# Mixer weight sums by accumulating transfers in DRAM, product banks alternated, operands fetched in double steps

## The chip, the cores and the metric

The kernel runs on one core of one Trainium2 chip. The metric is the device time of one execution in microseconds. A kernel is run several times and the median is given.

The core's engines each work through their own queue in order: PE (TensorE) does matmuls and transposes, DVE (VectorE) and ACT (ScalarE) elementwise work, POOL (GpSimd) elementwise work too, SP (SyncE) issues transfers. Engines wait for one another by semaphores. A DMA that an engine issues stands in that engine's queue until what it waits for has come.

## The reference, cut to what matters

One block on 1024 tokens of width 1024: an S5 state-space branch and a forgetting-attention branch, merged by gates, then one output projection, a cross-attention into 256 memory tokens, a SwiGLU feed-forward and norms.

```python
u = rms_norm(h, norm_mix)
u_ssm, q, k, v, f_logit, gate_logits = split(u @ w_in)
y_ssm = gelu(s5_ssm(u_ssm, ...))
glu_a, glu_b = split(y_ssm @ w_glu, 2)
out_a = glu_a * sigmoid(glu_b)
out_b = forgetting_attention(q, k, v, f_logit + b_forget) @ w_fox_o
gate_a, gate_b = split(sigmoid(gate_logits), 2)
h = h + (gate_a * out_a + gate_b * out_b) @ w_mix_out
h = h + memory_cross_attention(rms_norm(h, norm_mem_q), rms_norm(mem, norm_mem_kv), ...)
f_a, f_b = split(rms_norm(h, norm_ffn) @ w_ffn_in, 2)
h = h + (silu(f_a) * f_b) @ w_ffn_out
return rms_norm(h, norm_final)
```

The change concerns the line with `w_mix_out`, a product of 1024x1024 by 1024x1024, and what is prepared beside it.

## The kernel before, in words

All matrix products are done on fp32 values split in two: a rounded high part and the rest as low part. ACT casts the high part (L183) and DVE or POOL subtracts to get the low part (L184). One product of 128x128 by 128x512 is three matmuls: high by high, high by low, low by high. Small tiles are named `whi`/`wlo`, `moh`/`mol`, `wph`/`wpl` for such pairs.

The program's stages in order: the input norm and projections with the S5 branch, attention, the gated unit, the products of the output projection, cross-attention, feed-forward, final norm. What follows is what the change and the prediction touch. Line numbers are those of the kernel before, as in its profile.

*The start.* Tokens are normed, `w_in` is loaded by SP in pieces (`raw`, L158), the S5 inputs are stored to DRAM (`u_d<-us`, L515) and read back regrouped (`xg<-u_d`, L1594). POOL scales two token tiles (`xt`, L229) and then makes the S5 weights: `w`, `fre`, `fim` (L1523 to L1526), which PE transposes at L1569, powers `EC`, `ES` (L1555 to L1557), and small constants such as `r` (L1603) and `St` (L1632).

*The gated unit.* For each of eight blocks `j` of 128 channels, `Glu` makes `glu_a` by DVE (`sg<-mm`, L1328), the sigmoid of `glu_b` by ACT (`sb`, L1333), their product by DVE (L1334), and POOL multiplies by the gate `ga` that SP loads (`sg<-sg,ga`, L1341). `fox_part(j)` makes the attention's projection on PE in `pv` or `misc` banks (three matmuls, L173 to L175), multiplies it by the gate `gb` on DVE (L617) and adds (L620). Half tiles (`ga`, `gb`, `sb`) come from a small pool that is reused.

*The output projection* is Strassen's in Winograd's form. The merged activations and `w_mix_out` are cut into 2x2 blocks of 512x512, and seven products of blocks, numbered 1 to 7, are added into `H`, which holds `x` at first. The activation sums are made on DVE in `merged_pair` (L636 to L641). The weight sums for products 4 to 7 are made in the gated unit: `mix_fetch` loads rows of `w_mix_out`, `mix_sums` adds on POOL (L654), `mix_store` writes the sums to the DRAM tile `mt_d` (L659). Each product has four steps of 128 rows of the inner dimension (`p`), each step 4 x 3 matmuls of 128x512 (L703) that accumulate in four PSUM banks; behind the fourth step four DVE operations add the banks into `H` (L710). `m_get` fetches a step's operands: it loads one weight block (128x512) into `raw`, and splits the activation block with DVE and the weight block with POOL. The order of products is 1, 6, 7, 5, 4, 2, 3; product 1, 6, 5 use the banks sc, sc, mm, mm, products 7 and 4 use mm, misc, pv, pv, products 2 and 3 go by tiles or by the first set. Operands are fetched four steps ahead.

*Beside the products*, `ahead(j)` prepares tiles of the feed-forward weight `w_ffn_in`: SP loads two tiles (`wpr`), ACT and DVE split them, DVE makes five sums (L793 to L798), and ACT's queue stores the results to DRAM (`w_d`, L771). `ahead(0)` is woven among the products' steps, then come `ahead(1)` and `ahead(2)`, beside the last products, the norms and what follows.

*Order.* A scheduler places each instruction in its engine's queue by the order in the code, by what it depends on and by its own estimate, so what depends on nothing can stand far ahead of where the code writes it. `issue_after` (in `B.behind`) holds an instruction back.

Of the kernel before, what the change touches and what calls it, by code (L numbers as in the profile page):

```python
# [9 lines left out]
F32 = mybir.dt.float32  # L10
# [9 lines left out]
P = 128  # L20
# [289 lines left out]
def hybrid_block_kernel(ctx: ExitStack, tc: tile.TileContext, x, mem, norm_mix, w_in, b_forget,  # L310
# [30 lines left out]
    wg_d = B.dram.tile([4, P, 2 * D], F32, name="wg_d")  # L341
    glu = Glu(B, sh, yT, wg_d, gate_d)
    with tc.tile_pool(name="fox", bufs=1, reuse_waits="tile") as fp:
        fox = Fox(B, fp, sh, uT, w_in, b_forget[0], cum_d, rd_d, att_d)
        fox.run(y_d, yT, aT, w_glu, wg_d, [f for j in range(4) for f in glu.values(j)])
    glu.after = fox.maxima[NH - 2]
    with tc.tile_pool(name="st2", bufs=1, reuse_waits="tile") as s2:
        stage_tail(B, big, s2, sh, x, glu, aT, gate_d, kv_d, w_fox_o, w_mix_out, norm_mem_q[0], w_mem_q,
                   w_mem_o, norm_ffn[0], w_ffn_in, w_ffn_out, norm_final, out)
# [232 lines left out]
def stage_tail(B, big, s2, sh, x, glu, aT, gate_d, kv_d, w_fox_o, w_mix_out, g_mq, w_mem_q, w_mem_o, g_ffn,  # L582
# [7 lines left out]
    def slot(dt=F32, name="t"):  # L590
        return s2.tile([P, D], dt, tag="t", bufs=NS2, name=name)
# [10 lines left out]
    mt_d = B.dram.tile([8, 4, P, 512], F32, name="mt_d")  # L602
    mblk = {}

    def fox_part(j):
# [15 lines left out]
        if j % 2 == 0:  # L621
            gs[j // 2] = sg[:, :512]
        else:
            merged_pair(j // 2)

    def block(n, p):


        if p % 2 == 0 and (n, p) not in mblk:
            t_ = slot(name=f"m{n}")  # L630
            mblk[n, p], mblk[n, p + 1] = t_[:, :512], t_[:, 512:]
        return mblk[n, p]

    def merged_pair(p):
# [3 lines left out]
        V.tensor_sub(block(7, p), a11, a21)  # L638
# [3 lines left out]

    msum = {}

    def mix_fetch(p):
        msum[p] = slot(name="ws1"), slot(name="ws2")
        for i, t_ in enumerate(msum[p]):
            S.dma_start(t_, w_mix_out[(2 * p + i) * P:(2 * p + i + 1) * P, :])

    def mix_sums(p):  # L650
        w1, w2 = msum[p]
        b11, b12, b21, b22 = w1[:, :512], w1[:, 512:], w2[:, :512], w2[:, 512:]
        for o, i in ((b11, b12), (b12, b22), (b22, b11), (b21, b22)):
            G.tensor_add(o, o, i)  # L654

    def mix_store(p):
        w1, w2 = msum.pop(p)
        for n, o in ((5, w1[:, :512]), (7, w1[:, 512:]), (6, w2[:, 512:]), (4, w2[:, :512])):
            S.dma_start(mt_d[n, p], o)  # L659

    for j in range(8):
        if j > 3:
            with B.behind(glu.after):
                for f in glu.values(j):
                    f()
        glu.rest(j)
# [6 lines left out]
        if j > 2:  # L673
            fox_part(j - 3)
    H = [bslot(name=f"h{t}") for t in range(NT)]
    u2 = Act(s2, "t", NS2, 8, L, name="u2")
    MORDER = (1, 6, 7, 5, 4, 2, 3)
    mseq = [(n, p) for n in MORDER for p in range(4)]
    mops = {}

    def m_get(m):
        n, p = mseq[m]
        rb = B.wpool.tile([P, RAW], F32, tag="raw", bufs=4, name="raw")[:, :512]
        if n < 4:
            j, c = 2 * p + (n > 1), 512 * (n > 2)
            src = w_mix_out[j * P:(j + 1) * P, c:c + 512]
        else:
            src = mt_d[n, p]
        S.dma_start(rb, src)
        if m < 4:  # L690
            hl = [B.wpool.tile([P, WSLOT], F32R, tag=t_, name=t_)[:, :D] for t_ in ("whi", "wlo")]
        else:
            hl = bslot(F32R, "moh"), bslot(F32R, "mol")
# [4 lines left out]
    def m_mm(m, i, ps):  # L698
        n, p = mseq[m]
        hi, lo = mops[m]  # L700
        gi = slice(i * P, (i + 1) * P)
        for k, (l_, r_) in enumerate(((hi, hi), (hi, lo), (lo, hi))):
            T.matmul(ps, l_[:, gi], r_[:, 512:], start=k == 0 and p == 0 and n in (1, 2, 7),  # L703
                     stop=p == 3 and k == 2, skip_group_check=True)

    def m_add(n, i, ps):
        t, c, op = {1: (4, 0, ALU.add), 2: (4, 0, ALU.add), 6: (0, 0, ALU.add), 7: (0, 1, ALU.subtract),
                    5: (0, 1, ALU.subtract), 4: (0, 0, ALU.add), 3: (4, 1, ALU.subtract)}[n]
        h = H[t + i][:, 512 * c:512 * c + 512]
        return V.tensor_tensor(out=h, in0=h, in1=ps, op=op)  # L710

    msets = []

    def m_step(m):
        n, p = mseq[m]
        if m == 0:
            msets.append([B.bank(t_) for t_ in ("sc", "sc", "mm", "mm")])
        if m == 8:
            msets.append([B.bank(t_) for t_ in ("mm", "misc", "pv", "pv")])
        set_ = msets[n in (7, 4)]  # L720
        for i in range(4):
            m_mm(m, i, set_[i])
        if p == 3:
            for i in range(4):
                m_add(n, i, set_[i])

    def m_tile(i):
        ps = B.bank(("mm", "misc")[i % 2])
        for p in range(4):
            m_mm(20 + p, i, ps)  # L730
        m_add(2, i, ps)

    def m_x(t):
        S.dma_start(H[t], x[t * P:(t + 1) * P, :])

    MAHEAD = 4
    for t in range(4, NT):
        m_x(t)
    fox_part(5)
    for m in range(3):  # L740
        m_get(m)
    fox_part(6)
    m_get(3)
    m_step(0)
    m_step(1)
    for t in range(4):
        m_x(t)
    fox_part(7)
    m_get(4)
    m_get(5)  # L750
    gq = B.bcast_gain(s2, g_mq)

    def gemm_n(ps, act, t, w, nk):
        for k in range(nk):
            ah, al = act.tok(k, t)
            B.mm3(ps, ah, al, w[0][k], w[1][k], k == 0, k == nk - 1)

    def norm(t, gb, act, banks=("misc", "pv")):
        xs = s2.tile([P, D], F32, tag="xs", bufs=1, name="xs")
        B.norm_scale(xs, H[t], B.rstd(H[t]), gb)  # L760
        return B.norm_turn(xs, act, t, banks)

# [5 lines left out]
    def ahead(j):  # L768
# [53 lines left out]

    def m_next(m):
# [843 lines left out]
class Fox:  # L1667
# [280 lines left out]
    def run(self, y_d, yT, aT, w_glu, w_d, filler):  # L1948
# [54 lines left out]
        for h in range(NH):  # L2003
# [76 lines left out]
```

## Time and profile before

| | us |
|---|---|
| median of three runs | 1553.93 |
| the three runs | 1553.87, 1553.93, 1557.8 |
| the profiled execution | 1555.15 |
| its span in the trace | 1553.4 |
| PE busy in the span | 1518.3 |
| DVE busy | 1043.6 |
| ACT busy | 670.3 |
| POOL busy | 318.4 |
| PE's granted clock, mean | 0.993 of full |

The span is the traced part of the execution; 1.75 us of the profiled time lie outside it. A busy share is an average over stages with different limits, so the stretch from 540 to 800 us, in which the gated unit and the products run, is read by itself.

In rows of groups or lines of code, `L703 PE MATMUL sc<-moh` says: line 703, engine, operation, the tile written and the tile read. PEld is PE's loading of weights. A row of waits says which engine at which line waited, for which engine's work at which line, with total, count and longest wait in us. A row of the chain of waits gives the start, the duration and the work that something later waited for.

### The profile page before, as it was taken

What the parts mean: (1) busy time and instruction counts of PE and PEld (TensorE: products, weight loads), DVE (VectorE), ACT (ScalarE), POOL (GpSimd) and SP (SyncE); (2) the same over time, 40 slices, a digit from 0 to 9 for tenths busy, and PEclk for the clock granted to TensorE, in tenths of its full rate; (3) what the DMA queues carried; (4) which work ended last, traced back from release to release, by engine and by line L of the source; (5) the groups of instructions that cost most, each with busy time, mean ns of one, the idle gap of its engine ahead of it and who ended that gap; (6) DMA issues with size and microseconds to landing.
All of it is one profiled execution on the core that took longest, in us unless ns stands there. A gap on an engine that the chain in (4) does not pass through costs nothing.

```text
span 1553.4 us, 20548 instructions
## 1 busy us (share of the span) xinstructions
PE 1518.3 (98%) x7281; PEld 1251.6 (81%) x7281; DVE 1043.6 (67%) x1860; ACT 670.3 (43%) x1215; POOL 318.4 (20%) x385
## 2 busy tenths in 40 slices
PE   8999999999999997999899999999999999999998
PEld 7888888898777676887778888888888888888886
DVE  7936463346788855778866697777777776576555
ACT  7423333324667642124655564333333333354343
POOL 1166541100121218424402200000000000101001
PEclk9999999999999999999999999999999999999999
DMA  9734556611233747676630256445555543897652
GB/s 282 161 107 96 135 124 139 195 28 11 50 49 84 210 133 249 209 256 209 210 121 4 109 191 197 162 160 158 159 160 160 160 149 129 276 393 238 190 162 109
DMA packets 200454, 245.60 MB, mean 158 GB/s; under 512 B 36152, under 2 KB 128232, under 8 KB 199840
## 3 DMA queue, kind: packets, MB, share of 16 engines
q1 hardware_dynamic: 192864, 226.47, 49.0%
q10 hardware_dynamic: 7488, 17.83, 3.1%
q8 instruction: 57, 0.93, 0.2%
q14 instruction: 45, 0.37, 0.1%
HBM read 169.28 MB, written 76.91 MB: 158 GB/s over the span
## 4 chain that ended last, share of the span: by engine, by line
PE 84%; DVE 7%; DMA 3%; ACT 2%; issue 2%; POOL 2%; SPq 0%; POOLq 0%; ACTq 0%; DVEq 0%
PE mm L1054 15%; PE pv L1054 8%; PE mm L173 7%; PE mm L175 7%; PE mm L174 7%; PE mm L1197 5%; PE sc L1054 4%; PE sc L1197 4%; PE pv L1197 3%; PE sc L175 3%; PE sc L174 3%; PE sc L173 3%; PE misc L1197 2%; PE mm L703 1%; PE sc L1882 1%
## 5 line engine op out<-in xcount | busy, mean ns | idle before, releaser
L183 ACT CAST whi<-raw 128x1024 fp32r<-128x1024 f32 (+2 forms) x120 | 107.1, 895 | 112.2 <-PE mm L174 39.1
L184 DVE TENSOR_TENSOR wlo<-raw,whi 128x1024 fp32r<-128x1024 f32 (+2 forms) x116 | 121.7, 1055 | 40.4 <-ACT whi L183 39.3
L184 DVE TENSOR_TENSOR ol<-or,oh 128x1024 fp32r<-128x1024 f32 x73 | 92.2, 1267 | 71.9 <-ACT oh L183 71.1
L173 PE MATMUL mm<-uh,whi 128*128 128x512 f32 x344 | 136.5, 397 | 0.0
L174 PE MATMUL mm<-ul,whi 128*128 128x512 f32 x344 | 135.1, 393 | 0.0
L175 PE MATMUL mm<-uh,wlo 128*128 128x512 f32 x344 | 134.5, 391 | 0.0
L183 ACT CAST oh<-or 128x1024 fp32r<-128x1024 f32 x73 | 76.8, 1053 | 104.7 <-PE mm L1197 34.1
L1087 POOL TENSOR_TENSOR g<-a,c 128x512 f32<-128x512 f32 x22 | 35.7, 1621 | 389.8 <-ACT a L1086 369.8
L1892 POOL TENSOR_TENSOR pl<-pf,ph 128x512 fp32r<-128x512 f32 (+1 forms) x32 | 36.9, 1153 | 232.1 <-DVE ph L1891 193.3
L175 PEld LDWEIGHTS mm<-uh,wlo 128*128 128x128 f32 x344 | 64.7, 188 | 13.3 <-DVE wlo L184 0.2
L173 PEld LDWEIGHTS mm<-uh,whi 128*128 128x128 f32 x344 | 64.8, 188 | 11.5
L174 PEld LDWEIGHTS mm<-ul,whi 128*128 128x128 f32 x344 | 64.8, 188 | 11.0
L1076 DVE SCALAR_TENSOR_TENSOR c<-c,pv 128x512 f32<-128x512 f32 x22 | 15.1, 687 | 77.0 <-ACT c L1075 76.9
L1889 ACT ACTIVATE pf<-sc 128x512 f32<-128x512 f32 (+1 forms) x96 | 46.4, 489 | 44.5 <-DVE sc L1885 28.6
L211 POOL TENSOR_TENSOR r<-ms,mhalf 128x1 f32<-128x1 f32 (+1 forms) x26 | 16.5, 640 | 219.1 <-DVE ms L207 178.1
L1054 PE MATMUL pv<-S3h,we 128*128 128x512 f32 x176 | 57.7, 389 | 0.0
L184 POOL TENSOR_TENSOR mol<-raw,moh 128x512 fp32r<-128x512 f32 x24 | 37.1, 1558 | 43.2 <-ACT moh L183 30.3
L1895 DVE TENSOR_TENSOR pl<-pf,ph 128x512 fp32r<-128x512 f32 (+2 forms) x64 | 35.2, 553 | 10.2 <-ACT ph L1894 9.6
L1197 PE MATMUL mm<-ol,oh 128*128 128x512 f32 (+1 forms) x110 | 41.9, 381 | 0.0
L1197 PE MATMUL mm<-oh,ol 128*128 128x512 f32 (+1 forms) x110 | 41.9, 381 | 0.0
L1197 PE MATMUL mm<-oh 128*128 128x512 f32 (+1 forms) x110 | 41.9, 381 | 0.0
L173 PE MATMUL mm<-yh,whi 128*128 128x512 f32 x104 | 41.1, 395 | 0.0
(663 smaller groups left out, 4665.4 us busy)
## 6 DMA issues: line engine op xcount, KB each, us to landing
or<-c_d SPq DMA_DIRECT2D x77, 256.0 KB
wo<-in_w_ffn_out_dram SPq DMA_DIRECT2D x22, 512.0 KB
c_d<-g SPq DMA_DIRECT2D x44, 256.0 KB
t_d<-wo SPq DMA_DIRECT2D x44, 256.0 KB
or<-t_d SPq DMA_DIRECT2D x44, 256.0 KB
rawb<-in_w_ffn_in_dram SPq DMA_DIRECT2D x20, 512.0 KB
raw<-in_w_ffn_in_dram SPq DMA_DIRECT2D x20, 512.0 KB
raw<-in_w_in_dram SPq DMA_DIRECT2D x19, 512.0 KB
```

What stands on the lines that cost most here:

```text
L173: T.matmul(ps, lh, rh, start=first, stop=False)
L174: T.matmul(ps, lh, rl, start=False, stop=False)
L175: return T.matmul(ps, ll, rh, start=False, stop=last)
L183: cast = self.A.copy(hi, src)
L184: self.rest = (self.G if pool_lo else self.V).tensor_sub(lo, src, f32(hi))
L211: self.G.tensor_tensor(out=r, in0=v, in1=self.mhalf[:, 0:n], op=ALU.pow)
L1054: T.matmul(ps, l_[:, k, :], r_, start=first and k == 0 and i == 0, stop=k == 3 and i == 2, skip_group_check=True)
L1087: G.tensor_mul(g[:, 512:], a1, c1)
L1197: T.matmul(ps, l_[:, gi], r_[:, c0:c1], start=k == 0 and (p == NP - LAST if own else p == 0 and n in (1, 2, 7)), stop=p == NP - 1 and k == ...
L1889: self.exp = A.activation(pf[:, off:], ps[:, off:], AF.Exp)
L1892: G.tensor_sub(pl[:, off:], pf[:, off:], f32(ph[:, off:]))
L1895: self.left = V.tensor_sub(pl[:, off:], pf[:, off:], f32(ph[:, off:]))
```

## The change

1. `mix_sums` becomes a list of steps outside `stage_tail`: SP copies blocks of `w_mix_out` to `mt_d`, and POOL issues transfers from `w_mix_out` that add to what is in `mt_d` (`accum_op`). Product 6's sum is a copy of 5's with one more added, 4's a copy of 6's with one more. The steps are handed to attention, one to each of heads 1 to 6. `mix_fetch`, POOL's adds and `mix_store` go.
2. The order of products is 1, 7, 6, 4, 5, 2, 3, so that neighbours use different sets of banks.
3. `m_get(d)` fetches two steps at once: one transfer of two blocks, operands of 128x1024, both low parts by DVE. It runs two double steps ahead.
4. `ahead(0)` is done beside the gated unit (at `j` = 0, 2, 3, 4, 5), with tiles from the stage's own pool.
5. The activation difference for product 7 is made when the even block of a pair is ready.

```diff
+def mix_sums(B, w, mt_d):
+    S, G = B.S, B.G
+    blk = w.rearrange("(p two k) (c n) -> two c k p n", two=2, k=P, c=2)
+    dst = {n: mt_d[n].rearrange("p k n -> k p n") for n in (4, 5, 6, 7)}
+    def add(n, i, j):
+        for p in (0, 2):
+            G.dma_start(dst[n][:, p:p + 2], blk[i, j, :, p:p + 2], accum_op=ALU.add)
+    return [lambda: (S.dma_start(dst[5], blk[0, 0]), S.dma_start(dst[7], blk[0, 1])),
+            lambda: (add(5, 0, 1), add(7, 1, 1)),
+            lambda: S.dma_start(dst[6], dst[5]), lambda: add(6, 1, 1),
+            lambda: S.dma_start(dst[4], dst[6]), lambda: add(4, 1, 0)]
...
         if j % 2 == 0:
             gs[j // 2] = sg[:, :512]
+            V.tensor_sub(block(7, j // 2), block(1, j // 2), gs[j // 2])
...
-        for o, i in ((b11, b12), (b12, b22), (b22, b11), (b21, b22)):
-            G.tensor_add(o, o, i)
...
-            S.dma_start(mt_d[n, p], o)
...
+    first = ahead(0, lambda name, dt=F32: slot(dt, name))
     for j in range(8):
...
         glu.rest(j)
-        if j < 4:
-            mix_fetch(j)
-        if 0 < j < 5:
-            mix_sums(j - 1)
-        if 1 < j < 6:
-            mix_store(j - 2)
+        if j in (0, 2, 3, 4, 5):
+            first.pop(0)()
         if j > 2:
             fox_part(j - 3)
...
-    MORDER = (1, 6, 7, 5, 4, 2, 3)
+    MORDER = (1, 7, 6, 4, 5, 2, 3)
...
-        B.split(hl[0][:, :512], hl[1][:, :512], mblk[n, p])
-        B.split(hl[0][:, 512:], hl[1][:, 512:], rb, True)
-        mops[m] = hl
+        S.dma_start(raw.rearrange("k (p c) -> k p c", p=2), src)
+        hl = []
+        for src in (mblk[n, p], raw):
+            if d > 11:
+                hl.append((slot(F32R, "moh"), slot(F32R, "mol")))
+            elif d % 4 < 2:
+                hl.append([B.wpool.tile([P, WSLOT], F32R, tag=t_, name=t_)[:, :D] for t_ in ("whi", "wlo")])
+            else:
+                hl.append((bslot(F32R, "moh"), bslot(F32R, "mol")))
+            B.split(*hl[-1], src)
+        mops[d] = hl
...
-        if m == 8:
+        if m == 4:
             msets.append([B.bank(t_) for t_ in ("mm", "misc", "pv", "pv")])
...
-        if m + MAHEAD < len(mseq):
-            m_get(m + MAHEAD)
-    weave([lambda m=m: m_next(m) for m in range(2, 20)], ahead(0), 4)
+        if m % 2 and m // 2 + 2 < 14:
+            m_get(m // 2 + 2)
+    for m in range(2, 20):
+        m_next(m)
...
+            elif h < 7:
+                side[1].append(sums[h - 1])
```

How instructions stand in the engines' queues, as built. First PE, at the passage from product 1 to the next one; `whi`, `wlo` are product 1's operands, `moh`, `mol` the next one's, and the name ahead of the arrow is the bank. Before:

```order
L703 MATMUL mm<-whi 128x512
L703 MATMUL mm<-wlo,whi 128x512
L703 MATMUL mm<-whi,wlo 128x512
L703 MATMUL sc<-moh 128x512
L703 MATMUL sc<-mol,moh 128x512
```

Now:

```order
L761 MATMUL mm<-whi 128x512
L761 MATMUL mm<-wlo,whi 128x512
L761 MATMUL mm<-whi,wlo 128x512
L761 MATMUL mm<-moh 128x512
L761 MATMUL mm<-mol,moh 128x512
L761 MATMUL mm<-moh,mol 128x512
L761 MATMUL misc<-moh 128x512
```

Before, product 6 begins in product 1's own `sc` banks; now product 7 begins in the other set, in a third `mm` bank and in `misc`.

Next POOL in the gated unit; `ws` are rows of `w_mix_out`, `sg` and `ga` the gated unit's value and gate. Before:

```order
L1341 TENSOR_TENSOR sg<-sg,ga 128x512 x4
L654 TENSOR_TENSOR ws_6040<-ws_6040 128x512
L654 TENSOR_TENSOR ws_6040<-ws_6040,ws_6041 128x512
L654 TENSOR_TENSOR ws_6041<-ws_6041,ws_6040 128x512
L654 TENSOR_TENSOR ws_6041<-ws_6041 128x512
L654 TENSOR_TENSOR ws_6082<-ws_6082 128x512
L654 TENSOR_TENSOR ws_6082<-ws_6082,ws_6083 128x512
L654 TENSOR_TENSOR ws_6083<-ws_6083,ws_6082 128x512
L1341 TENSOR_TENSOR sg<-sg,ga 128x512
```

Now:

```order
L1891 TENSOR_TENSOR pl<-pf,ph 128x256
L1891 TENSOR_TENSOR pl<-pf,ph 128x512 x3
L1340 TENSOR_TENSOR sg<-sg,ga 128x512 x16
L211 TENSOR_TENSOR r_7289<-ms_7288,mhalf 128x1
L211 TENSOR_TENSOR r_7358<-ms_7357,mhalf 128x1
```

All sixteen gate multiplies now follow the attention's work (`pl`) directly, and the splits of the products (`wlo`, `mol`) that stood behind them are gone from POOL; what follows is the norm's `r`.

Last SP and POOL near the program's start, where `raw` are pieces of `w_in` and `mt_d` the weight sums. SP before:

```order
L158 DMA raw<-in_w_in_dram 128x4x256 x4
L515 DMA u_d<-us 128x1024
L158 DMA raw<-in_w_in_dram 128x4x256
L515 DMA u_d<-us 128x1024
L158 DMA raw<-in_w_in_dram 128x4x256
L515 DMA u_d<-us 128x1024 x2
```

SP now:

```order
L158 DMA raw<-in_w_in_dram 128x4x256 x3
L594 DMA mt_d<-in_w_mix_out_dram 128x4x512
L158 DMA raw<-in_w_in_dram 128x4x256
L594 DMA mt_d<-in_w_mix_out_dram 128x4x512
L596 DMA mt_d<-mt_d 128x4x512
L516 DMA u_d<-us 128x1024
L597 DMA mt_d<-mt_d 128x4x512
L516 DMA u_d<-us 128x1024
L158 DMA raw<-in_w_in_dram 128x4x256 x2
```

POOL before, where `w` and `fre` are the first S5 weights:

```order
L211 TENSOR_TENSOR r_653<-ms_652,mhalf 128x2
L229 TENSOR_TENSOR xt<-xt,gain 128x1024 x2
L1523 TENSOR_TENSOR w_1107<-ld_re,bb_re 128x448
L1524 TENSOR_TENSOR w_1108<-ld_im,bb_im 128x448
L1526 COPY fre<-bb_re 128x4x16
```

POOL now:

```order
L229 TENSOR_TENSOR xt<-xt,gain 128x1024 x2
L592 DMA mt_d<-in_w_mix_out_dram 128x2x512 x8
L1522 TENSOR_TENSOR w_1107<-ld_re,bb_re 128x448
L1523 TENSOR_TENSOR w_1108<-ld_im,bb_im 128x448
L1525 COPY fre<-bb_re 128x4x16
```

The four copies and the eight accumulating transfers, which the code writes in attention, stand at the end of the input stage: on SP between the loads of `w_in` and the stores of `u_d`, on POOL between the scaling of `xt` and the S5 weights. Before, neither queue had any of them there.

More of the change, by code (lines that the diff above doesn't have):

```diff
@@ L698, in m_mm @@
[L698 to L710, printed above, removed]
@@ L733, in m_x @@
[L733 to L756, printed above, removed]
@@ new lines, in m_x, with gemm_n, norm @@
+    def m_x(t):
+        S.dma_start(H[t], x[t * P:(t + 1) * P, :])
+    fox_part(5)
+    m_get(0)
+    m_x(4)
+    m_x(5)
+    fox_part(6)
+    m_get(1)
+    m_x(6)
+    m_x(7)
+    m_step(0)
+    m_step(1)
+    fox_part(7)
+    m_get(2)
+    for t in range(4):
+        m_x(t)
+    gq = B.bcast_gain(s2, g_mq)
+    def gemm_n(ps, act, t, w, nk):
+        for k in range(nk):
+            ah, al = act.tok(k, t)
+            B.mm3(ps, ah, al, w[0][k], w[1][k], k == 0, k == nk - 1)
+    def norm(t, gb, act, banks=("misc", "pv")):
+        xs = s2.tile([P, D], F32, tag="xs", bufs=1, name="xs")
+        B.norm_scale(xs, H[t], B.rstd(H[t]), gb)
+        return B.norm_turn(xs, act, t, banks)
```

127 lines of the change are left out of this document (59 added, 68 removed).

## The prediction

> **What bounds the kernel now.** I read the page's busy shares first, then PE's list of waits between 540 and 800 us, where the edited code runs, then the busy time by stretches of 10 us, and last the chain of waits through the worst stretch.
>
> ```profile
> PE 1518.3 (98%) x7281; PEld 1251.6 (81%) x7281; DVE 1043.6 (67%) x1860; ACT 670.3 (43%) x1215; POOL 318.4 (20%) x385
> ```
>
> PE is busy in 98% of the span, so a change that keeps the matmuls (this one does: same 28 steps of 12) can only win where PE stands still or runs slowly, or lose by making it stand. PE's waits in the stretch, as total, times, longest:
>
> ```profile
> core 0 of [0], span 1553.4 us
> engine line waited for: us in total, times, longest us
> PE pv L173 <- DVE gb L617: 8.0, 1, 8.0
> PE mm L703 <- DVE h L710: 2.9, 1, 2.9
> PE sc L703 <- DVE h L710: 2.8, 1, 2.8
> ```
>
> Three waits: one in the gated unit (L173 computes the attention's output projection into a `pv` bank) and two among the seven products (L703). In the stretches that hold them the columns are PE, PEld, DVE, ACT and POOL busy with counts, then the granted clock, DMA share and GB/s:
>
> ```profile
> 600.00:610.00 10.00, 10.00 (x46) 8.28 (x45) 2.27 (x2) 0.73 (x1) 9.69 (x9) 1.00 0.99 339
> 610.00:620.00 10.00, 3.54 (x16) 2.61 (x14) 4.09 (x3) 1.51 (x3) 9.77 (x7) 0.85 0.47 181
> 620.00:630.00 10.00, 8.45 (x25) 6.75 (x26) 6.90 (x7) 0.00 (x0) 9.12 (x7) 0.64 0.58 196
> 700.00:710.00 10.00, 7.25 (x26) 5.51 (x25) 9.27 (x14) 0.83 (x2) 0.29 (x1) 0.83 0.28 102
> 750.00:760.00 10.00, 7.11 (x25) 5.41 (x24) 8.91 (x15) 7.04 (x16) 4.39 (x4) 0.83 0.92 310
> ```
>
> The granted clock falls with each wait, so a stall costs more than its idle time. How much, I take from counts of matmuls against the undisturbed pace, which the chain of waits gives beside a slowed dozen:
>
> ```profile
> 753.38 4.57 PE mm L703 x12
> 757.95 2.72 PE misc L703 x12
> ```
>
> 12 in 2.72 us is 0.227 us each, 44.1 in 10 us. Stall A (610 to 630) ran 16 + 25 = 41 where 88.2 fit: 47 missing, 10.7 us. Stall B (700 to 710) ran 26: 18 missing, 4.1 us. Stall C (750 to 760) ran 25: 19 missing, 4.3 us. Together 19.1 us. Of the idle time 8.0 + 2.8 + 2.9 = 13.7 us are waits; the other 5.4 are the slow clock. [...]
>
> What A waits for, in the chain of waits (start, us, what):
>
> ```profile
> 600.37 1.26 POOL ws L654
> ...
> 609.47 1.26 POOL sg L1341
> 610.73 2.24 POOL ws L654
> ...
> 617.56 1.27 POOL sg L1341
> ...
> 621.55 0.80 PE pv L173
> ```
>
> POOL adds weight blocks (`ws`, L654, 16 in all) in the same queue as the gate multiplies (`sg`, L1341) that the gated unit needs, and POOL is 9.7 of 10 busy. From 610.73 to 617.56 it does sums while the multiply that PE lacks stands behind them; from 600.37 to 609.47 the same.
>
> B and C have one cause: product 6 accumulates in the banks that product 1 has just left, so its first matmul needs four adds into `h`:
>
> ```profile
> 704.30 1.27 DVE L710 TENSOR_TENSOR h<-h,sc 128x512 f32<-128x512 f32 x2
> ...
> 705.12 0.47 PE L703 MATMUL sc<-moh 128*128 128x512 f32 x1 [2.75 <-DVE h L710]
> ```
>
> **The change part by part.** *POOL's sums go.* 16 operations of 1.26 to 2.24 us leave POOL between 596 and 627. The multiply at 617.56 loses 6.8 us of sums directly ahead of it (610.73 to 617.56) and up to 9.1 us ahead of the one before (600.37 to 609.47); PE needs it 8.0 us earlier. That is 15.9 against 8.0, so A's cover is some 8 us. Against it stands new work: `first`, the preparation of the feed-forward weights, moves here, on DVE 5 adds, 4 low parts of 128x512 and one of 128x1024, about 9 × 0.69 + 1.2 = 7.4 us, with casts and stores in ACT's queue. ACT evicts the sigmoids behind those casts and stores, and a store waits for DVE's low part. DVE is 2.27 of 10 busy at 600 to 610, so 7.4 us fit there; if all of it landed ahead of the one multiply, the cover would be nearly used. I take A as gone (10.7); bounds 0 and 10.7.
>
> *The banks alternate.* Product 7 follows product 1 in the other set (mm, misc, pv, pv), 6 returns to the first, then 4, 5. The four adds now have a whole product, 4 × 2.72 = 10.9 us, before their bank is wanted, where they had none; B and C waited under 3. Both go unless DVE falls a whole product behind: 8.4 us; bounds 0 and 8.4.
>
> *Double steps.* Operands are split two at a time, all low parts on DVE, none on POOL:
>
> ```profile
> 690.00:760.00 70.00, 64.36 (x269) 52.36 (x268) 62.22 (x78) 33.26 (x61) 31.24 (x21) 0.95 0.63 206
> L184 DVE TENSOR_TENSOR mol<-m,moh 128x512 fp32r<-128x512 f32 x20 | 17.8, 888 | 4.2 <-ACT moh L183 4.2
> L184 DVE TENSOR_TENSOR mol<-m,moh x20: 676/693/1782, 693.3 to 755.8; 128x512 fp32r<-128x512 f32 x20
> L184 DVE TENSOR_TENSOR wpl<-wpr,wph 128x512 fp32r<-128x512 f32 x8 | 9.0, 1143 | 0.8 <-ACT wph L183 0.7
> L184 POOL TENSOR_TENSOR mol<-raw,moh x20: 1267/1458/2360, 693.9 to 755.2; 128x512 fp32r<-128x512 f32 x20
> L184 DVE TENSOR_TENSOR wlo<-raw,whi x11: 1203/1215/2050, 587.1 to 786.3; 128x1024 fp32r<-128x1024 f32 x11
> ```
>
> DVE is busy 62.2 of these 70 us. It loses 20 × 0.888 = 17.8 and gains 20 of 128x1024 at 1.215 = 24.3. `first` takes one of the two preparations out of here: half the `wpl` row, 4.5, and five sums at about the same 1.143, 5.7. Net 24.3 - 17.8 - 10.2 = -3.7, so 58.5 us of DVE in at least 60 us of matmuls if DVE's operations stay as slow as now. They should not: the same form takes 0.69 at the median and up to 1.78 where POOL works beside it (the mean of 1.143 mixes both), and POOL has no splits left; I reckon 50 to 55. A double step lasts 5.45 us of PE and wants 2 × 1.215 of splits plus on average 1.4 of adds into `h`, 3.8 in all, with a lookahead of two. The products' loads (two blocks at once), the order of the loads of `x` and the subtraction for product 7, done half a pair earlier, cost nothing: DMA and DVE do the same work. Cost 0, with some 2 us for a first wait or a changed tail; bounds -3 (the norms and transposes after 760 lose some 3 us now) and +8.4 (new waits as large as B and C).
>
> *The sums in DRAM.* Neither product stage nor attention holds them in the built order. Nothing precedes them, so they stand at the start of POOL's and SP's queues: four copies of 1 MB on SP, eight accumulating transfers of 512 KB on POOL. They chain: copy 5, add 5, copy 6, add 6, copy 4, add 4. POOL can't pass the issue of add 4, and behind it is the S5 branch's first POOL work; on SP the stores `u_d` and two weight loads stand behind copies 6 and 4.
>
> ```profile
> 80.40 1.17 POOL L1523 TENSOR_TENSOR w<-ld_re,bb_re 128x448 f32<-128x448 f32 x1 [31.41 <-DVE bb_re L1477]
> ...
> 93.68 0.11 POOL L1603 MEMSET r<- 128x4 f32 x1 [4.86 <-ACT r L1602]
> 95.89 0.11 POOL L1632 MEMSET St<- 128x8 f32 x1 [2.11 <-DMA u_d<-us]
> ...
> 96.73 1.16 POOL L1525 TENSOR_TENSOR fim<-w,w 128x448 f32<-128x448 f32 x1
> 110.60 1.05 ACT L183 CAST whi<-raw 128x1024 fp32r<-128x1024 f32 x1 [1.90 <-DMA gate_d<-gs]
> L1569 PE MATMUL pv<-ident,fre x16: 270/272/273, 113.4 to 252.2; 128*128 128x128 f32 x16
> 60.00:65.00 5.00, 5.00 (x25) 4.22 (x25) 4.83 (x39) 1.11 (x3) 0.00 (x0) 1.00 0.98 206
> 298.00:308.00 10.00, 10.00 (x85) 9.96 (x83) 2.63 (x7) 2.66 (x5) 0.00 (x0) 1.00 0.98 368
> ```
>
> POOL has idled 31.4 us when it starts at 80.4. From there to the end of `fim` (97.9) it is idle 4.9 + 2.1 us, which a late start absorbs: it needs 10.5 us. PE wants the result at 113.4, so POOL may start as late as 102.9. The copies of `w_glu` into DRAM ran at 368 GB/s (298 to 308): 1 MB in 2.9 us, about 5 with issue and landing. The first two stand among the loads issued before 60 and share a full DMA (0.98 busy, 206 GB/s at 60 to 65): 2 MB from 58 at that rate land at about 68. With `a` us for an accumulate of 1 MB, POOL is free at 68 + a + 5 + a + 5 = 78 + 2a. No row shows an accumulating transfer. Below, it costs a copy, 2.9; above, the present route for the same MB (2 MB loaded, 1 MB stored, 3 MB at the 339 GB/s of 600 to 610, = 9, and four POOL sums of about 1.6) 15. I take 6, near the copy but with both operands read: free at 90, hidden, cost 0; copy 4 has then left SP by about 85, and the loads behind it are cast at 110.6. At 2.9 it is 84; at 15 it is 108, 5 us past the cover. [...]
>
> Sum: -10.7 - 8.4 + 2 = -17.1. The profiled execution took 1555.15 us (1.75 outside the span), 1.2 above the median of 1553.93. It becomes 1538.0, and a median 1536.8: 1537.
>
> **The rivals.** *The accumulates hold up the start (slower).* If `a` passes 12.5 us, PE stands at L1569; every further us costs two. The gain of 17 is used up at a = 21, and 30 us each make POOL free at 138, a stall of 35: 1537 + 35 = 1572. [...] Against it: 1 MB in 21 us would be 50 GB/s, a seventh of the copies' rate. [...]
>
> *The gated unit still waits.* ACT's stores and casts for `first`, or DVE's 7.4 us, take the place of POOL's sums in front of the sigmoid's eviction: only B and C go, 1553.9 - 8.4 = 1545.5. For it: that evictor is in the chain of A. Against it: DVE 2.27 of 10 busy at 600.
>
> *DVE becomes the bound of the products.* Late splits instead of late banks: only A goes, 1553.9 - 10.7 = 1543. For it: 62 of 70 busy now. Against it: the sum above.
>
> *It doesn't do what it says.* The sums are not spread through attention but stand at the start; that is so in the order, and it costs only by the first rival.
>
> **How the numbers follow.** All three stalls go and the start is covered: 0.50, 1534 to 1540. Gated unit still waits: 0.12. DVE bound: 0.13. The start is held up: 0.18, of which 0.04 still faster, 0.03 level, 0.11 slower. A wait elsewhere that I don't see: 0.07, 0.03 level and 0.04 slower. A difference of 0.3%, 4.7 us, is about what a measurement of this kernel can tell. Faster 0.50 + 0.12 + 0.13 + 0.04 = 0.79, same 0.06, slower 0.15. The range runs from all stalls and 3 us of the tail regained (1553.9 - 19.1 - 3 = 1531) through both partial gains to a gain of 3 (1551); above it lie the held-up start and the unseen wait.
>
> **What would show it.** Right: PE without waits and at clock 1.00 from 610 to 630 of the old time, no L768 `h` among PE's releasers, POOL's first S5 work between 84 and 103, PE unbroken at 113. Wrong: PE waiting for POOL's `fre` or for `xg` before 130; an ACT `sb` or DVE `gb` ahead of PE in the gated unit; PE waiting for DVE's `mol`, or for `whi` from a late load, in the products.

## The result, and the profile after

The changed kernel takes 1581.06 us at the median (1580.27 to 1582.09 in 4 runs), against 1554.14 for the kernel before: ratio 1.0168, 95% interval 1.015 to 1.0186. It is 27 us slower, where 17 us less was forecast. The profiled execution's span is 1578.0 us. All medians and ratios count runs at a granted clock of 0.98 of full or more; one run, of the order of products alone, took 2076.78 us at a clock of 0.678 and is left out of them.

The page's first part, then PE's list of waits over the whole span, its four largest:

```profile
PE 1519.8 (96%) x7281; PEld 1255.2 (80%) x7281; DVE 1039.0 (66%) x1860; ACT 669.5 (42%) x1187; POOL 259.9 (16%) x349
```

```profile
PE pv L1568 <- POOL ES L1547: 26.5, 1, 26.5
PE pv L1651 <- ACT Tt L1586: 5.9, 1, 5.9
PE pv L1568 <- POOL fim L1524: 3.8, 1, 3.8
PE mm L173 <- DVE sg L1327: 3.8, 1, 3.8
```

PE's busy time is the same (1519.8 us, before 1518.3); it stands still more. None of the three waits of before is left: the wait for `gb` and both waits for the adds into `h` are gone. Three new ones lie near the program's start (L1568 is the transpose of POOL's S5 weights; the first row names `ES`, a small fill that stands right behind `fre` in POOL's queue), a fourth in the gated unit. The stretches that hold the first ones:

```profile
100.00:110.00 10.00, 10.00 (x46) 8.29 (x45) 0.00 (x0) 0.60 (x1) 1.15 (x1) 1.00 0.68 105
110.00:120.00 10.00, 3.45 (x16) 2.52 (x14) 0.00 (x0) 0.00 (x0) 1.15 (x1) 0.87 0.45 77
120.00:130.00 10.00, 0.00 (x0) 0.00 (x0) 0.00 (x0) 0.00 (x0) 1.15 (x1) 0.50 1.04 290
130.00:140.00 10.00, 0.04 (x1) 0.04 (x1) 0.00 (x0) 2.75 (x4) 4.63 (x9) 0.50 0.84 188
140.00:150.00 10.00, 6.16 (x26) 5.67 (x27) 1.37 (x2) 1.51 (x3) 9.61 (x21) 0.50 0.37 102
```

PE is still from about 113 to 144 us, its clock falls to 0.50, and DVE has nothing to do from 100 to 140. Here is what POOL does in that time, by its timeline (start, us, what, and in brackets the idle time before it and what ended it):

```profile
74.72 1.36 POOL L592 DMA_DIRECT2D mt_d<-in_w_mix_out_dram  x1 [25.75 <-DMA mt_d<-in_w_mix_out_dram]
81.28 1.17 POOL L592 DMA_DIRECT2D mt_d<-in_w_mix_out_dram  x1 [5.20 <-issue]
87.78 1.15 POOL L592 DMA_DIRECT2D mt_d<-in_w_mix_out_dram  x1 [5.34 <-issue]
98.37 1.16 POOL L592 DMA_DIRECT2D mt_d<-in_w_mix_out_dram  x1 [9.44 <-issue]
104.90 1.15 POOL L592 DMA_DIRECT2D mt_d<-in_w_mix_out_dram  x1 [5.37 <-issue]
110.77 1.15 POOL L592 DMA_DIRECT2D mt_d<-in_w_mix_out_dram  x1 [4.72 <-issue]
123.59 1.15 POOL L592 DMA_DIRECT2D mt_d<-in_w_mix_out_dram  x1 [11.67 <-DMA mt_d<-mt_d]
135.37 1.15 POOL L592 DMA_DIRECT2D mt_d<-in_w_mix_out_dram  x1 [10.63 <-issue]
136.09 1.44 POOL L1522 TENSOR_TENSOR w<-ld_re,bb_re 128x448 f32<-128x448 f32 x1
```

The eight accumulating transfers, and nothing else, fill POOL's queue from 74.7 to 136.1. Of the seven gaps between them one is a wait for a copy; the profile puts the other six down to no other engine ("issue"): there each transfer was issued 5.9 to 11.8 us after the one before it, which is about when that one had landed, 6.3 us after its issue at the median (5.6 to 11.5). The S5 weights begin at 136.1 in place of 80.4.

The rest of the program gained about what was forecast. The last store of the S5 branch's `yh` is issued at 333.9 us (before: 289.1), 44.8 later; the feed-forward's first `pv` product stands at 960.5 (before: 936.1), 24.4 later. Between them the changed kernel gained 20.4 us. The products run from 723.9 to 809; up to 790 a view shows no idle PE and full clock:

```profile
690.00:790.00 100.00, 100.00 (x447) 82.90 (x446) 86.32 (x109) 43.30 (x58) 7.62 (x7) 1.00 0.66 224
```

### The profile page after: what moved, and what is told of

Read it like the earlier page. It is cut to its first block, busy times and chain, and to the rows that moved or that the text cites. A ratio compares the mean times of both kernels' runs of the same rounds, so it can differ in the third digit from the quotient of the medians.

```text
span 1578.0 us, 20402 instructions
## 1 busy us (share of the span) xinstructions
PE 1519.8 (96%) x7281; PEld 1255.2 (80%) x7281; DVE 1039.0 (66%) x1860; ACT 669.5 (42%) x1187; POOL 259.9 (16%) x349
## 4 chain that ended last, share of the span: by engine, by line
PE 79%; DVE 7%; issue 5%; DMA 4%; POOL 2%; ACT 2%; SPq 0%; ACTq 0%; POOLq 0%; DVEq 0%
PE mm L1053 15%; PE pv L1053 8%; PE mm L173 6%; PE mm L175 6%; PE mm L174 6%; PE mm L1196 5%; PE sc L1053 4%; PE sc L1196 4%; PE pv L1196 3%; PE sc L173 2%; PE sc L175 2%; PE sc L174 2%; PE mm L761 2%; PE misc L1196 2%; DMA mt_d<-in_w_mix_out_dram 1%
## 5 line engine op out<-in xcount | busy, mean ns | idle before, releaser
L183 ACT CAST whi<-raw 128x1024 fp32r<-128x1024 f32 (+2 forms) x122 | 111.0, 913 | 105.3 <-PE mm L174 36.2
L184 DVE TENSOR_TENSOR wlo<-raw,whi 128x1024 fp32r<-128x1024 f32 (+2 forms) x122 | 128.7, 1060 | 39.1 <-ACT whi L183 36.4
L174 PE MATMUL mm<-ul,whi 128*128 128x512 f32 x344 | 136.1, 396 | 0.0
L173 PEld LDWEIGHTS mm<-uh,whi 128*128 128x128 f32 x344 | 65.5, 190 | 11.8
L1539 DVE TENSOR_TENSOR Gm<-w,w 64x512 f32<-64x512 f32 x8 | 5.5, 683 | 66.4 <-POOL w L1534 66.4
L1894 DVE TENSOR_TENSOR pl<-pf,ph 128x512 fp32r<-128x512 f32 (+2 forms) x64 | 35.3, 553 | 10.3 <-ACT ph L1893 9.6
```

The costliest lines, as they stand in the source:

```text
L173: T.matmul(ps, lh, rh, start=first, stop=False)
L174: T.matmul(ps, lh, rl, start=False, stop=False)
L183: cast = self.A.copy(hi, src)
L184: self.rest = (self.G if pool_lo else self.V).tensor_sub(lo, src, f32(hi))
L1894: self.left = V.tensor_sub(pl[:, off:], pf[:, off:], f32(ph[:, off:]))
```

## The experiments

Theory Q: the whole loss is POOL's in-order queue, held by the chain of sums ahead of work that PE needs soon; everything else in the change gains some 21 us. The rivals are that the transfers cost as much wherever they stand (T), that SP's queue does it (S), and other readings of single steps, named with each run. The three kernels that leave additions out and the one with sixteen transfers were run once each. Ratios and medians stand beside the runs of the kernel before on the same chip.

### Held in attention, as the code has it

```diff
-                side[1].append(sums[h - 1])
+                side[1].append(lambda f=sums[h - 1], m=self.maxima[h]: held(f, m))
```

> The changed kernel, with each of the six steps of the weight sums held back until the row maxima of the attention head beside which the code writes it. Theory Q (the 45 us between the input stage and the end of the S5 branch are lost because POOL, and SP behind it, stand at the front of their queues for the accumulating transfers, and nothing else went wrong): the S5 branch ends at about 291 us as before the change, the rest keeps its gain of 21, total 1536, 1533 to 1540. Rival T (the transfers cost as much wherever they stand: POOL is blocked some 8 us for each pair, and the low parts `pl` of the probabilities wait behind it): PE waits in attention, up to 30 us in all, total 1545 to 1570.

1554.78 us against 1552.93: ratio 1.0009, interval 0.9999 to 1.0019. The rival T held: the start is as before the change, and attention loses what the products gain. POOL's timeline and two of PE's waits there:

```profile
399.60 1.36 POOL L592 DMA_DIRECT2D mt_d<-in_w_mix_out_dram  x1 [7.86 <-DMA mt_d<-in_w_mix_out_dram]
406.48 1.19 POOL L592 DMA_DIRECT2D mt_d<-in_w_mix_out_dram  x1 [5.52 <-DVE mc L1856]
407.20 1.22 POOL L1891 TENSOR_TENSOR pl<-pf,ph 128x256 fp32r<-128x256 f32 x1
```

```profile
PE mm L1851 <- DVE mc L1856: 3.9, 3, 2.8
PE pv L1913 <- POOL pl L1891: 3.4, 1, 3.4
```

From 391.7 to 407.2 POOL does nothing but wait for a copy and issue the two transfers of one sum, while `pl`, the low part of a head's probabilities, stands behind them. So the sums cost some 22 us (1554.8 against the 1532 to which the chain fits below) where the code means them to stand, too.

### Without the adds

```diff
-            G.dma_start(dst[n][:, p:p + 2], blk[i, j, :, p:p + 2], accum_op=ALU.add)
+            pass
```

> The changed kernel without the eight accumulating transfers; the four copies stay at the start on SP. It leaves the additions out of four of the weight sums. Theory Q: POOL starts the S5 weights at 80 us, PE has no wait at the transposes of `fre`, the total is 1536. Rival S (SP's queue is what holds the start, by the copies ahead of the stores of `u_d` and the loads of `w_in`): PE still waits before 130 us for `xg` or for a cast of `raw`, the total stays above 1545.

1531.41 us, one run. Q held. S fell as far as the copies themselves go: they stay at the start of SP's queue and cost nothing when they needn't wait for adds.

```profile
81.13 1.17 POOL L1522 TENSOR_TENSOR w<-ld_re,bb_re 128x448 f32<-128x448 f32 x1 [31.41 <-DVE bb_re L1476]
```

```profile
PE mm L173 <- DVE sg L1327: 1.0, 1, 1.0
```

So the adds cost 1581 - 1531 = 50 us where the change has them, and all the rest of it gains 1552.9 - 1531.4 = 21.5. By the traces 44.1 us of the loss are there at the last store of `yh` (333.9 against 289.8). Another 4.5 come between it and the feed-forward's first product (626.6 us against 622.1), where the gated unit's wait for `sg` is 3.8 us in the change and 1.0 here.

### The same transfers from POOL, without adding

```diff
-            G.dma_start(dst[n][:, p:p + 2], blk[i, j, :, p:p + 2], accum_op=ALU.add)
+            G.dma_start(dst[n][:, p:p + 2], blk[i, j, :, p:p + 2])
```

> The changed kernel with the eight transfers issued by POOL as before but overwriting in place of adding. It leaves the additions out of four of the weight sums. What spaces them 5.9 to 11.8 us apart? Theory W (POOL's own writing of the requests, whatever the transfer does): the spacing stays at 6 us or more and the total at 1575 to 1582. Theory A (reading, adding and writing in the transfer, with the next one started only when the last has landed): the spacing falls to between 1.2 and 4 us, POOL is free by 90 to 105 us, the total is 1536 to 1542.

1552.98 us. The spacing followed theory A, the total didn't:

```profile
72.69 1.60 POOL L592 DMA_DIRECT2D mt_d<-in_w_mix_out_dram  x2 [22.81 <-DMA mt_d<-in_w_mix_out_dram]
80.46 1.38 POOL L592 DMA_DIRECT2D mt_d<-in_w_mix_out_dram  x2 [6.17 <-DMA mt_d<-in_w_mix_out_dram]
89.84 1.37 POOL L592 DMA_DIRECT2D mt_d<-in_w_mix_out_dram  x2 [8.00 <-DMA mt_d<-mt_d]
102.06 1.38 POOL L592 DMA_DIRECT2D mt_d<-in_w_mix_out_dram  x2 [10.85 <-DMA mt_d<-mt_d]
103.46 1.01 POOL L1522 TENSOR_TENSOR w<-ld_re,bb_re 128x448 f32<-128x448 f32 x1
```

```profile
PE pv L1651 <- ACT Tt L1586: 9.3, 1, 9.3
PE mm L173 <- DVE sg L1327: 4.4, 1, 4.4
PE pv L1568 <- POOL fim L1524: 1.3, 1, 1.3
```

Plain transfers go out two in 1.4 to 1.6 us: POOL's own part in issuing them, 0.69 us each at the median, isn't what spaces the adds. But with POOL free at 103.5, just past the point that the prediction called covered, the kernel is 21.6 us above the run without the adds. 14.9 us of that are there at the last store of `yh` (304.7 against 289.8). POOL's timeline further on:

```profile
114.17 0.11 POOL L1631 MEMSET St<- 128x8 f32 x1 [4.19 <-DMA u_d<-us]
115.01 1.13 POOL L1524 TENSOR_TENSOR fim<-w,w 128x448 f32<-128x448 f32 x1
```

POOL stands still again until the stores of `u_d` have landed, which wait behind copy 4 on SP: the last is issued at 99.6 (before the change: 93.1), and POOL goes on at 114.2 (before: 95.9), with the transfer engines full in between (a share of 1.03 at 100 to 110). So what stands on SP does bear on the start, as S says, once its copies wait for POOL's transfers. The wait for `fim` is 1.3 us; the one that costs is the next, for `Tt` at L1651, further down the same S5 quarter. The other 6.5 us (628.6 us from the last store of `yh` to the feed-forward's first product, against 622.1) come in the gated unit, where the wait for `sg` is 4.4 us here and 1.0 there.

### Half the bytes in as many pieces

```diff
-            G.dma_start(dst[n][:, p:p + 2], blk[i, j, :, p:p + 2], accum_op=ALU.add)
+            G.dma_start(dst[n][:, p:p + 2, :256], blk[i, j, :, p:p + 2, :256], accum_op=ALU.add)
```

> The changed kernel, its accumulating transfers cut to the left 256 of 512 columns of each row: as many pieces, half the bytes of each. It leaves the additions out of the other half of the sums. What makes one of these transfers last some 6.5 us? Theory bytes: the spacing in the quiet parts falls to 3.5 to 4.5 us, POOL is free some 20 us earlier, total 1558 to 1564. Theory pieces (each row of a block costs the same whatever its length): the spacing stays near 6.5, total 1577 to 1582.

1570.66 us, between the two. The quiet spacings:

```profile
79.93 1.17 POOL L592 DMA_DIRECT2D mt_d<-in_w_mix_out_dram  x1 [4.00 <-issue]
84.43 1.15 POOL L592 DMA_DIRECT2D mt_d<-in_w_mix_out_dram  x1 [3.33 <-issue]
```

4.5 us here, 5.9 (104.90 to 110.77) with twice the bytes. If the time grows evenly with the bytes, an estimate from these two spacings is that 256 KB of adding cost 1.4 us, and that some 3.1 us came on top of each transfer of 256 pieces with only one out.

### Sixteen transfers of 256 KB

```diff
-        for p in (0, 2):
-            G.dma_start(dst[n][:, p:p + 2], blk[i, j, :, p:p + 2], accum_op=ALU.add)
+        for p in range(4):
+            G.dma_start(dst[n][:, p:p + 1], blk[i, j, :, p:p + 1], accum_op=ALU.add)
```

> The changed kernel with its adds in sixteen transfers of 256 KB in place of eight of 512 KB, all else and all places as in the change. Why is the next one not issued before the last has landed? Theory O (so much is outstanding with one of 512 KB that a second has no room): smaller ones are issued several at a time, POOL is free 12 to 25 us earlier, total 1556 to 1568. Rival E (each adding transfer waits for the one before it, whatever its size, at a fixed 3 us and 1.4 us for each 256 KB): sixteen times 4.5 and more, POOL is free after 140 us, total above 1585.

1562.64 us: theory O held.

```profile
72.06 2.73 POOL L592 DMA_DIRECT2D mt_d<-in_w_mix_out_dram  x3 [23.09 <-DMA mt_d<-in_w_mix_out_dram]
79.32 0.84 POOL L592 DMA_DIRECT2D mt_d<-in_w_mix_out_dram  x1 [4.53 <-issue]
80.61 0.82 POOL L592 DMA_DIRECT2D mt_d<-in_w_mix_out_dram  x1 [0.45 <-issue]
```

Three go out in 2.7 us, the fourth after a gap of 4.5. Of 512 KB only one went out at a time, 5.9 us apart and more. If a limit on what POOL may have outstanding is behind this, as theory O has it, one add of 512 KB took more than half of it; the runs show the counts, not the limit.

### The order of products alone

```diff
-    MORDER = (1, 6, 7, 5, 4, 2, 3)
+    MORDER = (1, 7, 6, 4, 5, 2, 3)
...
-        if m == 8:
+        if m == 4:
```

> The kernel before, with one part of the change alone: the order of products 1, 7, 6, 4, 5, 2, 3, with the second set of banks taken at product 7. Theory B (the two waits of PE for the adds into `h` come from the banks being reused at once): both waits go, 1554.1 - 8.4 = 1546, 1543 to 1548. Rival D (they come from DVE being behind, with POOL's splits slowing it): PE waits as long for `mol` or for later adds, 1550 to 1556.

1553.96 us against 1552.93: ratio 1.0007, interval 0.9997 to 1.0016. The rival D held. Stall B is gone, but the products stand still 40 us later:

```profile
700.00:710.00 10.00, 10.00 (x46) 8.29 (x45) 9.97 (x15) 2.12 (x4) 1.32 (x2) 1.00 0.37 123
740.00:750.00 10.00, 8.24 (x33) 5.64 (x31) 9.29 (x11) 7.68 (x15) 6.34 (x4) 1.00 0.66 207
750.00:760.00 10.00, 6.72 (x18) 4.65 (x19) 8.90 (x14) 3.04 (x7) 2.39 (x3) 0.66 0.75 273
```

```profile
PE mm L703 <- DVE mol L184: 3.1, 2, 1.7
PE sc L703 <- POOL mol L184: 1.2, 1, 1.2
```

51 matmuls ran from 740 to 760 where 88 fit: 37 missing, 8.4 us, now for want of `mol`, which POOL and DVE make. Stall B's 4.1 us have been added to stall C's 4.3.

### The chain in POOL's idle window

```diff
+        with B.tc.issue_after(loaded.ins):
+            sums[0]()
...
+        with B.behind(self.ones_set):
+            sums[1]()
```

Here `sums[0]` is the first two copies, `sums[1]` everything else, issued by POOL.

> The changed kernel with the chain of sums placed where POOL and the transfer engines are idle: the first two copies behind the last loads of the S5 branch on SP, the other two copies and all eight accumulating transfers on POOL behind its last constant of the attention's set-up, at about 293 us, 82 us ahead of its first work in attention. Theory Q (the only fault of the change is which work the serial chain stands ahead of): the chain of some 60 us fits, the total is that of the kernel without the adds, 1530 to 1534. Rival T (the chain is slowed by the four copies of `w_glu` beside it and ends after 375 us, or its transfers delay loads): PE waits in the first heads, 1535 to 1545.

1546.82 us (1537.72 to 1550.32 in 6 runs) against 1554.07: ratio 0.9942, interval 0.9921 to 0.9963. Rival T, a little above its range. The first add waits to 312.4 for the copies, which stand beside those of `w_glu` (before, the transfer engines were 0.98 busy at 298 to 308, while those ran); the last is issued at 388.5, 13 us past POOL's first work in attention, and here the transfers followed one another after up to 13.3 us:

```profile
312.35 1.36 POOL L592 DMA_DIRECT2D mt_d<-in_w_mix_out_dram  x1 [18.25 <-DMA mt_d<-in_w_mix_out_dram]
325.66 1.20 POOL L592 DMA_DIRECT2D mt_d<-in_w_mix_out_dram  x1 [11.95 <-issue]
...
388.53 1.15 POOL L592 DMA_DIRECT2D mt_d<-in_w_mix_out_dram  x1 [4.88 <-issue]
```

### The same, with the old order of products

```diff
-    MORDER = (1, 7, 6, 4, 5, 2, 3)
+    MORDER = (1, 6, 7, 5, 4, 2, 3)
...
-        if m == 4:
+        if m == 8:
```

> The same as the run with the chain in POOL's idle window, but with the products in the order of the kernel before (1, 6, 7, 5, 4, 2, 3) and the second set of banks taken at its product 7. Theory B (reusing a bank at once costs PE its wait whatever DVE does): the waits for the adds into `h` are back, 5 to 9 us more than with the new order, 1536 to 1541. Theory D (PE waits only where DVE is behind; with POOL's splits and one preparation gone it isn't): no more than 2 us above the new order, 1530 to 1534.

1546.69 us, ratio 0.9954, interval 0.9939 to 0.9969. Beside 1546.82 that is no difference, though each spreads over some 13 us, so the profile has to carry it. In the products PE's only wait for the adds is this:

```profile
PE mm L770 <- DVE h L777: 0.3, 1, 0.3
```

D again: with double steps, without POOL's splits and with one preparation less in the products, DVE isn't behind, and then taking a bank at once costs 0.3 us. The alternation that the forecast gave 8.4 us is worth about nothing by itself, in either kernel.

### The sums alone

The kernel before, with POOL's adds replaced by the chain in the idle window.

```diff
-        if 0 < j < 5:
-            mix_sums(j - 1)
...
+        with B.behind(self.ones_set):
+            sums[1]()
```

> The kernel before, with the weight sums alone taken from POOL's adds to the chain in its idle window; the products, their splits and the feed-forward preparation stay as they were. Theory A (the wait of 8.0 us in the gated unit and the slow clock behind it come from POOL's adds ahead of the gate multiplies): that wait goes, the two waits in the products stay, 1553 - 10.7 = 1542, 1540 to 1545. Rival: another engine holds the gated unit, or the products wait longer in turn: 1547 to 1553.

1554.31 us against 1554.07, ratio 1.0003, interval 0.999 to 1.0016: that is outside both ranges, and by itself decides nothing, since the chain costs attention here about what it cost in the last two runs. The trace takes the two apart: the last loads of the attention's output (`ath`) are issued at 573.6, 10.3 us later than before, and from there to the first matmul into an `mm` bank from `moh` it takes 132.5 us where it took 143.9. That is a gain of 11.4 in the gated unit and what follows up to there, where A says 10.7. The wait of the gated unit is gone from PE's list, and the products' two are as before:

```profile
PE mm L173 <- DVE mc L1856: 4.4, 1, 4.4
PE sc L705 <- DVE h L712: 2.8, 1, 2.8
PE mm L705 <- DVE h L712: 2.5, 1, 2.5
```

So stall A comes from POOL's adds, as theory A says, and B and C don't depend on it.

### A shorter chain in the idle window

```diff
+        for n, i, j in ((7, 0, 1), (5, 0, 0), (6, 0, 0), (4, 1, 0)):
+            S.dma_start(dst[n], blk[i, j])
...
+        add(7, blk[1, 1])
+        add_sum(6, 7)
+        add(5, blk[0, 1])
+        add_sum(4, 6)
```

> A shorter chain in POOL's idle window. All four copies come straight from the weight and stand at the start on SP, where copies alone cost nothing; the sum for product 6 is the sum for 7 plus a block, that for 4 the sum for 6 plus a block, so no copy stands between the adds. POOL issues the adds at about 293 us: those of 7 and 5 in transfers of 256 KB, those that add one sum to another in two of 512 KB with pieces of 4 KB. Theory Q: the chain ends by 345 us, 30 us ahead of POOL's first work in attention, and the total is that of the kernel without the adds, 1531, 1529 to 1534. Rival T: the adds beside the copies of `w_glu` and the loads of attention still cost PE waits there, 1535 to 1543.

1532.14 us against 1553.00: ratio 0.9861, interval 0.9844 to 0.9878. Q held.

```profile
293.87 2.50 POOL L592 DMA_DIRECT2D mt_d<-in_w_mix_out_dram  x3
307.39 0.84 POOL L592 DMA_DIRECT2D mt_d<-in_w_mix_out_dram  x1 [11.02 <-issue]
...
322.52 0.84 POOL L597 DMA_DIRECT2D mt_d<-mt_d  x1 [3.05 <-issue]
324.74 0.82 POOL L597 DMA_DIRECT2D mt_d<-mt_d  x1 [1.39 <-issue]
...
333.04 0.83 POOL L597 DMA_DIRECT2D mt_d<-mt_d  x1 [1.92 <-DMA mt_d<-mt_d]
376.19 0.74 POOL L1903 TENSOR_TENSOR pl<-pf,ph 128x256 fp32r<-128x256 f32 x1 [42.31 <-DVE ph L1902]
```

The last add goes out at 333.0, 42 us before POOL's first work in attention. Three things differ from the first chain in this window, and only together: the copies need no adds, no copy stands between the adds, and the transfers have fewer pieces. The two rows at L597 are of 512 KB each, in 128 pieces of 4 KB; these went out 2.2 us apart and landed 7.6 us after issue at the median, so two were out at once.

### With the feed-forward preparation back among the products

```diff
-    first = ahead(0, lambda name, dt=F32: slot(dt, name))
...
-        if j in (0, 2, 3, 4, 5):
-            first.pop(0)()
...
-    for m in range(2, 20):
-        m_next(m)
+    weave([lambda m=m: m_next(m) for m in range(2, 20)], ahead(0), 4)
```

> The same with one part of the change undone: the first preparation of the feed-forward weight is woven among the products again, as in the kernel before. Theory F (the wait of 1.0 to 4.7 us for DVE's copy into `sg` in the gated unit, seen in all runs that moved this preparation there, is its price): that wait goes, and the products, without POOL's splits, take the preparation without a wait: 2 to 4 us below the run beside it. Rival P (in the products it costs more, since DVE is 9 of 10 busy there): waits for `h` or `mol` are back, 2 to 8 us above the run beside it.

1530.69 us (1530.55 to 1531.32 in 4 runs), ratio 0.9855, interval 0.9841 to 0.987: the fastest of all. It is 1.4 us below the run beside it, less than theory F said, and the two sets of runs overlap, so the difference isn't shown. The wait of 1.1 us for `sg` in the gated unit is gone, and PE has no wait in the products. Rival P fell: there is room for the preparation among the products too.

## Why the prediction was wrong, by its steps

*POOL's sums go (10.7).* Right: the wait for `gb` is gone in the runs without POOL's adds, and the run with the sums alone gained 11.4 us there. A new wait stands there, for DVE's copy into `sg`: 3.8 us in the changed kernel. In the nine runs with `first` beside the gated unit it goes from none (sixteen transfers) to 4.7, though their code there is the same; with `first` back among the products it is gone. So `first` leaves room for it, and what sets its size stays open.

*The banks alternate (8.4) and double steps (-2).* Right as a sum, wrong as a cause. The products have no waits after the change. But alternation alone moves the stall, and double steps without alternation have none. What did it lies in the double steps; the preparation that was moved isn't needed for it, since PE has no wait in the products with it back there. The likeliest part is that POOL's splits are gone: DVE's split of 128x512 (`wpl`) took 1.143 us at the mean beside them and takes 0.684 without (690 to 760 in the last run); before, one at 711.65 took 1.80 us beside a split of POOL's (711.06 to 712.90) and one at 716.44, with POOL idle, 0.69. But DVE is no less busy in all (63.9 of 70 us at 660 to 730 there, 62.2 before), and no run takes the parts of the double steps apart. The forecast read "waits for `h`" as a need for another bank; with double steps the old order does without. Gated unit, products and what follows gained 20.4 us by the two traces, where 17.1 were forecast.

*The sums in DRAM (0).* This step failed: put at nothing, it cost 44.8 us by the end of the S5 branch. It had POOL free at 90 us; it was 136.1. By the timeline the difference of 46 us is made up so: the first copies landed at 74.7 in place of 68 (7); add 5 took 13.1 in place of 6 (7); add 7, which stands ahead of add 6 in POOL's queue and was left out of the chain, took 17.1, where only copy 6 with 5 was counted (12); add 6 took 12.1 in place of 6 (6); copy 4 6.6 in place of 5, which was the author's estimate (2); and the first half of add 4 held POOL for another 12.5, where the formula let it go at the copy (12). Under a third of the miss (13 of 46) is the price of an add, which was given bounds of 2.9 and 15 and measured 13.1 and 12.1. With these the formula, 78 + 2a, has POOL free at 102 to 104, at the edge of its cover: the price alone would have cost next to nothing. Most of the rest is the chain: the formula took the adds for transfers that are issued and left, and POOL had to stand by each.

By the estimate from the spacings of 4.5 and 5.9 us the price has two parts. 1.4 us for 256 KB is 5.6 us for 1 MB, twice the copies' 2.9: the bytes cost what the forecast took. The other 6 us are twice the 3.1 that each transfer took apart from its bytes with only one outstanding. With sixteen smaller ones, three out at once, some were issued only 1.3 us apart. In the idle window one of 512 KB held up the next for up to 13.3 us.

*The cover to 102.9 us.* This step failed too, in two ways. It was worked out for PE's transposes of `fim`, which before the change came 15.5 us behind it (97.9 to 113.4). A later consumer has less room: `Tt` is done by ACT at 141.3 there and used by PE at 145.1. And the stores of `u_d`, which the prediction saw behind the copies on SP but gave no price, hold POOL itself. The runs beside one another:

| run | POOL's first S5 work | its `fim` | last store of `yh` |
|---|---|---|---|
| before | 80.4 | 96.7 | 289.1 |
| without the adds | 81.1 | 97.9 | 289.8 |
| plain transfers | 103.5 | 115.0 | 304.7 |
| sixteen adds | 122.4 | 129.7 | 320.2 |
| half the bytes | 126.5 | 133.9 | 324.7 |
| the change | 136.1 | 143.6 | 333.9 |

Counted from `fim`, PE's end of the S5 branch is as late as POOL in all four late runs, less 1.6 to 2.7 us (18.3 and 15.6 in the third row, 46.9 and 44.8 in the last). Counted from POOL's start, the cover is 55.7 - 44.8 = 10.9 us in the change and 23.1 - 15.6 = 7.5 with plain transfers, where POOL stood still for `u_d`. So POOL could start as late as about 88 to 91, and the forecast's own 90 was at the edge. After `fim` POOL has another 13 us of work in that quarter and is 8.9 of 10 busy at 100 to 110 in the profile of before; the prediction took the next consumers one by one at their old times, and did not follow the chain from POOL by DVE's scans and ACT to L1651.

How much of the change's loss SP's queue would make by itself is not shown. There the last store of `u_d` is issued at 121.2 and its data is read back from 134.5 on; POOL comes to the work that needs it at 142.7. So POOL was the later of the two, by some 8 us, but both stood behind the same chain of adds, and every run that freed one freed the other.

*The rivals.* The one on the slower side had the right place, and its chance was 0.11. Its mechanism was right in part: POOL did stand by the adds, but it looked for the loss in the price of one, with a break-even of 21 us, and at 12 to 13 the gain was gone and more. The gated unit's rival was partly true (3.8 us). The spacing of the adds had little to do with DVE's load: it was 6.6 us with DVE 19.69 of 20 us busy (60 to 80) and 5.9 with DVE idle (100 to 120).

## What to carry to other kernels

Where an engine can't issue its next transfer before the last has landed, as POOL couldn't here with its adds of 512 KB (5.9 us apart and more), the transfer is work of that engine for as long: follow a chain of them through the queue, every entry, and ask what stands behind its last. A cover is the smallest over all who wait, found by moving the whole queue, not by one consumer. And a wait for a bank doesn't say that a bank is missing: ask why the engine that frees it is late, and try that by itself.

## What the runs showed of the hardware

- POOL issued one accumulating transfer of 512 KB (256 pieces of 2 KB) at a time, from 5.9 us apart (104.90 to 110.77 in the change) up to 13.3 (312.35 to 325.66 with the chain in the idle window); of 256 KB it had three out at once (2.7 us for three issues, with sixteen transfers). Plain ones of 512 KB went out two in 1.4 to 1.6 us.
- An accumulating transfer of 256 pieces between DRAM tensors, one out at a time, took 4.5 us at 256 KB and 5.9 at 512, spacing from issue to issue: an estimate from these two, if the time grows evenly with the bytes, is about 3.1 us and 1.4 for each 256 KB.
- How many were out went with the pieces more than with the bytes: at half the bytes in as many pieces there was still only one out at a time (4.5 us apart), and of 512 KB in 128 pieces of 4 KB two were out (322.52 and 324.74 in the shorter chain).
- Single waits of PE of 2.8 and 2.9 us stood in stretches of 10 us with a granted clock of 0.83 (before, 700 to 710 and 750 to 760); in the change, with PE still from 113 to 144, it was 0.50 from 120 to 150.
